# A hybrid decoder layer on one core: the first norm's token sums as single columns in another PSUM bank, and the transposes of the residual in pairs

## The chip, the core and the metric

The kernel runs on one core of a Trainium2 chip. TensorE (PE) multiplies matrices out of SBUF into PSUM, which has eight banks of 2 KiB a partition; VectorE (DVE), ScalarE (ACT) and GpSimd (POOL) do the elementwise work, and SyncE (SP) mainly issues DMA transfers. Each engine has its own stream of instructions, in a fixed order, and waits on semaphores. The metric is the device time of one execution in microseconds (us); lower is better.

## What is computed

One layer of a decoder for 512 tokens of width 2048, in float32:

```python
def hybrid_layer(x, ...):
    h = rmsnorm(x, norm1_w)
    proj = h @ w_in
    ...
    y_sb = stick_breaking_attention(heads(sb_q), heads(sb_k), heads(sb_v))
    y_sc = sc_b * causal_depthwise_conv(sc_c * sc_h, sc_conv_w)
    y_gdn = gdn_mixer(gdn_qkv, gdn_z, gdn_a, gdn_b, gdn_conv_w, gdn_a_log, gdn_dt_bias, gdn_norm_w)
    y = jnp.concatenate([y_sb.astype(x.dtype), y_sc, y_gdn], axis=-1)
    x = x + y @ w_out
    h2 = rmsnorm(x, norm2_w)
    return x + jnp.square(jax.nn.relu(h2 @ w_up)) @ w_down
```

A last rmsnorm follows. The three mixers are six heads of stick-breaking attention, four groups of a short gated convolution and six heads of a gated delta rule (GDN).

## The kernel before

The activations lie transposed in SBUF: 128 features on the partitions, 512 tokens along the free axis, 16 such tiles for the width of 2048. A float32 product is made of three fast ones: each operand is split into a rounded part (`hi`) and a rest (`lo`), and `mm3` (lines 116 to 118) issues hi·hi, hi·lo and lo·hi into one PSUM bank. A `gemm` of one 128-wide output tile is 16 steps of `mm3`, so 48 matmuls of 512 columns; its weights come in four chunks through `wload`: a DMA into `raw`, a cast by ACT into `whi` (line 103), a subtraction by DVE into `wlo` (line 104), with four buffers of each. The outputs of the gemms rotate over three banks named `mm`.

*First norm.* While x is loaded, ACT squares each tile and DVE adds the squares up in `acc` (128 x 512). The products with x run meanwhile without the norm, which is a factor for each token and is put in when results leave PSUM. The factor is wanted in two layouts. `R` (128 x 512, one column for each token, the same in all partitions) comes from one product of `ones` with `acc` (line 221) into the only bank of the tag `r`, and `rsqrt_exp`, two instructions on ACT (lines 146 and 148). `rtok` (128 x 4, tokens on the partitions) comes from four products of a 128-column block of `acc` with the whole matrix `ones` (line 226), again in the bank `r`, of which one column for each block is read. At this moment three gemms are finished and fill all three `mm` banks (`first`); the first of these leaves PSUM with line 344, `xp = p * R` on DVE, and the next gemm takes its bank.

*Mixers.* The GDN heads follow, each a chain of small matmuls (lines 361 to 544) between the many gemms of the input projection; then attention, which begins with `sb_qk(0)` and `sb_attn(0)`. There `sq` and `sk` are cast by ACT out of two `mm` banks (line 582), and the scores `z` are products of the two (lines 116 to 118 with outputs `z`). The last step of the last GDN head just before is line 544, four transposes on PE, whose result ACT scales into `y` (line 546).

*Output projection.* The loop over `m` runs 16 gemms with `wo`. After gemm m, DVE adds the residual and makes `x1[m]` (line 793). The residual is also wanted with tokens on the partitions; `turn(m)` (lines 774 to 777) makes four transposes of `x1[m]` into a bank of the tag `t` (two of them), copies them by ACT into half of the tile `turned`, and after an odd m sends both halves by one DMA to `xs` in DRAM. The loop calls `turn` for m-2 and m-1 ahead of gemm m for even m, and for 14 ahead of gemm 15.

*MLP.* The up and down projections follow, with an algorithm of seven products in place of eight, weights formed on DVE by additions. Its first weights (`q`, 512 KB each) are loaded into the space of the output projection's activations, so their DMAs start when its last gemm ends.

*Order.* Nobody writes the order of the instructions by hand. A scheduler takes instructions by priority (the code's order, with exceptions such as `tc.high_priority`) when their inputs are ready by its own reckoning of time, engine by engine; `behind(ins)` puts what is traced inside it behind `ins` on `ins`'s engine. A change in one place can thus move instructions far away.

Of the kernel before, what the change touches and what calls it, by code (L numbers as in the profile page):

```python
# [2 lines left out]

# [13 lines left out]
P = 128  # L17
T = 512
NB = T // P
D = 2048  # L20
KT = D // P
# [6 lines left out]
CHUNK_KT = 4  # L28
# [26 lines left out]
def trunk(ctx, tc, xT, wv1, wv2, wa, wo, wu, wd, vec, wf, out, dbg=None):  # L55
    nc = tc.nc
    V, S, G, PE = nc.vector, nc.scalar, nc.gpsimd, nc.tensor
# [15 lines left out]
    def mmps():  # L73
        pool, bufs = pool_of_mm
        return pool.tile([P, 512], F32, name="mm", tag="mm", bufs=bufs)

    def xps(tag):
        pool, bufs = pool_of[tag]
        return pool.tile([P, 512], F32, name=tag, tag=tag, bufs=bufs)
# [8 lines left out]
    def tmp(n=512):  # L88
        return per.tile([P, n], F32, name="tmp", tag="tmp", bufs=4)

    def big():
        return big_pool.tile([P, 2, 512], F32R, name="big", tag="big", bufs=16, align_bytes=256)

    def f32t(shape, name):
        return per.tile(shape, F32, name=name)

    def wload(src, n, prio=None):
        with tc.high_priority(WPRIO if prio is None else prio):
            raw = per.tile([P, 512], F32, name="raw", tag="raw", bufs=4)
            nc.sync.dma_start(out=raw[:, :n], in_=src)  # L100
            hi = per.tile([P, 512], F32R, name="whi", tag="whi", bufs=4, align_bytes=256)
            lo = per.tile([P, 512], F32R, name="wlo", tag="wlo", bufs=4, align_bytes=256)
            S.copy(out=hi[:, :n], in_=raw[:, :n])  # L103
            V.tensor_tensor(out=lo[:, :n], in0=raw[:, :n], in1=hi[:, :n].bitcast(F32), op=ALU.subtract)  # L104
        return hi, lo

    def behind(*ins):

        ctx = ExitStack()
        for i in ins:  # L110
            ctx.enter_context(tc.issue_after(i.ins))
        return ctx

    def mm3(p, lh, ll, rh, rl, first, last, more=False):

        PE.matmul(p, lhsT=lh, rhs=rh, start=first, stop=False, skip_group_check=more)  # L116
        PE.matmul(p, lhsT=lh, rhs=rl, start=False, stop=False, skip_group_check=more)  # L117
        return PE.matmul(p, lhsT=ll, rhs=rh, start=False, stop=last, skip_group_check=more)  # L118

    def gemm_chunk(p, src, acts, c, prio=None):  # L120

        ks = slice(c * CHUNK_KT, (c + 1) * CHUNK_KT)
        hi, lo = wload(src[:, ks, :].rearrange("p k f -> p (k f)"), CHUNK_KT * P, prio)
        for k in range(CHUNK_KT):
            s = slice(k * P, (k + 1) * P)
            a = acts[c * CHUNK_KT + k]
            mm3(p, hi[:, s], lo[:, s], a[:, 0], a[:, 1], c + k == 0, c * CHUNK_KT + k == KT - 1)

    def gemm(src, acts):
        p = mmps()  # L130
        for c in range(KT // CHUNK_KT):
            gemm_chunk(p, src, acts, c)
        return p

    def silu(x, s):
# [8 lines left out]
    def rsqrt_exp(o, i, scale, bias):  # L144

        S.activation(out=o, in_=i, func=AF.Ln, scale=scale, bias=eps_c)
        if bias is None:
            S.activation(out=o, in_=o, func=AF.Exp, scale=-0.5)
        else:
            S.activation(out=o, in_=o, func=AF.Exp, scale=-0.5, bias=bias)  # L150
# [8 lines left out]
    ones = f32t([P, P], "ones")  # L159
# [3 lines left out]
    def col(c):  # L163
        return vc[:, c:c + 1]
# [5 lines left out]
    def pt(shape, name, tag=None, bufs=1, dt=F32):  # L170
        return ph_pool.tile(shape, dt, name=name, tag=tag or name, bufs=bufs)
# [15 lines left out]
    acc = big_pool.tile([P, 512], F32, name="acc", tag="acc")  # L187
    pp0 = psum_pool("ps_v", v=4, r=1)
    v1p = [xps("v") for _ in range(NB)]
# [4 lines left out]
    for k in range(KT):  # L194
        hi, lo = wload(wv1[:, k, :], 268, 0)
        xr = big_pool.tile([P, 512], F32, name="xr", tag="xr", bufs=6)
        nc.sync.dma_start(out=xr, in_=xT[:, k, :])
        a = big()
# [4 lines left out]
        for b in range(NB):  # L203
            s = slice(b * P, (b + 1) * P)
# [15 lines left out]
    p = xps("r")  # L220
    PE.matmul(p, lhsT=ones, rhs=acc, start=True, stop=True)
    rsqrt_exp(R, p, 1.0 / D, None)
    rtok = pt([P, NB], "rtok")
    p = xps("r")
    for b in range(NB):
        PE.matmul(p[:, b * P:(b + 1) * P], lhsT=acc[:, b * P:(b + 1) * P], rhs=ones, start=True, stop=True)
    rsqrt_exp(rtok, p.rearrange("p (b f) -> p b f", b=NB)[:, :, 0], 1.0 / D, None)
    rtoks = pt([P, NB], "rtoks")
    S.mul(out=rtoks, in_=rtok, mul=SCALE)

# [84 lines left out]
    p = xps("r")  # L315
# [414 lines left out]
    yh = []  # L730
    for k in ORDER:
        a = big()
# [7 lines left out]
    def half_split(o, src):  # L740
        S.copy(out=o[:, :, 0], in_=src)
        V.tensor_tensor(out=o[:, :, 1], in0=src, in1=o[:, :, 0].bitcast(F32), op=ALU.subtract)
# [8 lines left out]
    def sums(o, A11, A12, A21, A22):  # L751

        sub(o[:, 0], A22, A21)
        nsub(o[:, 1], o[:, 0], A11)
        nsub(o[:, 2], o[:, 1], A12)
        sub(o[:, 3], A11, A21)
# [10 lines left out]
    def turn(m, p=None):  # L767

        if m % 2 == 0:
            turned["o"] = late.tile([P, NB, 2 * P], F32, name="turned", tag="turned", bufs=1)  # L770
        o = turned["o"]
        p = xps("t") if p is None else p
        for b in range(NB):
            PE.transpose(p[:, b * P:(b + 1) * P], x1[m][:, b * P:(b + 1) * P], ident)
        S.copy(out=o[:, :, m % 2 * P:m % 2 * P + P], in_=p.rearrange("p (b f) -> p b f", b=NB))
        if m % 2:
            nc.sync.dma_start(out=xs[:, :, (m - 1) * P:(m + 1) * P], in_=o)
# [7 lines left out]
    for m in range(KT):  # L785
        xr = big_pool.tile([P, 512], F32, name="xr", tag="xr", bufs=6)
        nc.sync.dma_start(out=xr, in_=xT[:, m, :])
        if m == KT - 1 or m and m % 2 == 0:
            for q in range(m - m % 2 - 2 + 2 * (m % 2), m):
                turn(q)  # L790
        p = gemm(wo[m], yh)
        x = big_pool.tile([P, 512], F32, name="x1", tag="xr", bufs=6) if m < KT - 1 else tmp()
        V.tensor_tensor(out=x, in0=p, in1=xr, op=ALU.add)
        y = tmp()
        S.activation(out=y, in_=x, func=AF.Copy, scale=col(C_N2 + m))
        if m == 0:
            S.activation(out=Rb, in_=x, func=AF.Square)
        else:
            sq = tmp()
            S.activation(out=sq, in_=x, func=AF.Square)  # L800
            if m < KT - 1:
                G.tensor_tensor(out=Rb, in0=Rb, in1=sq, op=ALU.add)
        x1.append(x)
        yw.append(y)
        i = m // 2
        half_split(XP[i][:, m % 2:m % 2 + 1], y[:, :HT].unsqueeze(1))
        if m % 2:
            t = xsum = late.tile([P, 4, HT], F32, name="xsum", tag="xsum", bufs=2)
            y0 = yw[m - 1]
            sums(t, y0[:, :HT], y[:, :HT], y0[:, HT:], y[:, HT:])  # L810
            if m < KT - 1:
                rows(i, t, y)
# [437 lines left out]
```

## Time and profile before

| | |
|---|---|
| time, median of 3 runs | 2168.53 us (2166.35 to 2169.36) |
| the profiled execution: its own time | 2170.97 us |
| the profiled execution: its span | 2169.3 us |
| PE busy | 2140.7 us (99%) |
| DVE busy | 1660.4 us (77%) |
| ACT busy | 1073.7 us (49%) |
| mean granted TensorE clock | 0.996 of full speed |

The span goes from the first instruction to the last of the profiled execution; its own time has 1.7 us more around it. Busy shares are means over stages with different limits: the first 740 us are the mixers with the input projection, 740 to 895 us the output projection, 895 to about 1540 us the up projection, and the rest the down projection and the last norm.

### The profile page before, as it was taken

The numbers are of one execution on the slowest core, as the hardware profiler recorded it, in microseconds if no ns is written. First come the engines' busy times: TensorE is split into PE (matmuls) and PEld (weight loads), VectorE is DVE, ScalarE is ACT, GpSimd is POOL, SyncE is SP. The second block draws the span as 40 slices with busy tenths as digits, with TensorE's granted clock in tenths as the row PEclk, the third lists the DMA queues.
The fourth block names the chain that finished last, engine by engine and source line by source line (L and its number), as shares of the span: only waits on it lengthen the run. The fifth ranks groups of instructions, "written<-read, shape, count | busy, mean of one in ns | idle before, by whom it ended". The sixth has DMA issues, their size and how long they took to land.

```text
span 2169.3 us, 33100 instructions
## 1 busy us (share of the span) xinstructions
PE 2140.7 (99%) x12674; PEld 1884.5 (87%) x12674; DVE 1660.4 (77%) x2360; ACT 1073.7 (49%) x1629; POOL 131.8 (6%) x188
## 2 busy tenths in 40 slices
PE   9999999999999999899999999999999999999998
PEld 8887888888988888799999999999878888888886
DVE  6678978644657755477888788778898898898897
ACT  5646666333445544444444454445544444454455
POOL 0000000000000011100000000000001000000101
PEclk9999999999999999899999999999999999999999
DMA  6333232322222354666666665666896877787674
GB/s 184 107 99 95 82 91 91 92 92 84 83 83 83 103 169 150 215 188 196 194 174 187 195 192 172 191 195 181 280 310 182 242 219 196 208 228 226 184 213 117
DMA packets 160719, 356.42 MB, mean 164 GB/s; under 512 B 20273, under 2 KB 62257, under 8 KB 160433
## 3 DMA queue, kind: packets, MB, share of 16 engines
q1 hardware_dynamic: 146304, 302.93, 41.4%
q0 software_dynamic: 13968, 50.86, 13.6%
q8 instruction: 99, 1.62, 0.3%
q14 instruction: 60, 0.48, 0.1%
q10 hardware_dynamic: 288, 0.52, 0.1%
HBM read 308.90 MB, written 45.36 MB: 163 GB/s over the span
## 4 chain that ended last, share of the span: by engine, by line
PE 92%; DVE 3%; DMA 2%; ACT 1%; issue 1%; SPq 0%; DVEq 0%; ACTq 0%
PE mm L117 10%; PE mm L116 10%; PE mm L118 10%; PE pu L118 10%; PE pu L116 10%; PE pu L117 10%; PE pp L117 9%; PE pp L118 9%; PE pp L116 9%; PE mm L280 1%; PE mm L281 1%; PE mm L279 1%; DMA ha<-hs 1%; DVE W L842 1%; DMA q<-in_wu_dram 0%
## 5 line engine op out<-in xcount | busy, mean ns | idle before, releaser
L841 ACT CAST W<-q 128x1024 fp32r<-128x1024 f32 x446 | 466.7, 1054 | 579.4 <-PE pp L118 258.0
L842 DVE TENSOR_TENSOR W<-q,W 128x1024 fp32r<-128x1024 f32 x446 | 540.9, 1221 | 134.8 <-ACT W L841 130.7
L116 PE MATMUL mm<-big,whi 128*128 128x512 f32 x1024 | 404.8, 396 | 1.3 <-ACT whi L103 0.6
L117 PE MATMUL mm<-big,whi 128*128 128x512 f32 x1024 | 403.9, 394 | 0.0
L118 PE MATMUL mm<-big,wlo 128*128 128x512 f32 x1024 | 402.5, 393 | 0.0
L117 PE MATMUL pp<-W,A 128*128 128x512 f32 x888 | 346.1, 390 | 1.0 <-DVE W L842 1.0
L118 PE MATMUL pp<-W,A 128*128 128x512 f32 x888 | 345.7, 389 | 0.4 <-DVE A L842 0.4
L116 PE MATMUL pp<-W,A 128*128 128x512 f32 x888 | 343.3, 389 | 1.4 <-ACT W L841 1.1
L104 DVE TENSOR_TENSOR wlo<-raw,whi 128x512 fp32r<-128x512 f32 (+1 forms) x292 | 196.6, 675 | 158.3 <-ACT whi L103 150.4
L103 ACT CAST whi<-raw 128x512 fp32r<-128x512 f32 (+1 forms) x292 | 177.3, 608 | 276.5 <-PE mm L117 239.0
L116 PE MATMUL pu<-XS,W 128*128 128x256 f32 x1024 | 288.4, 282 | 9.8 <-ACT W L841 9.6
L118 PE MATMUL pu<-XS,W 128*128 128x256 f32 x1024 | 287.7, 281 | 0.5 <-DVE W L842 0.5
L117 PE MATMUL pu<-XS,W 128*128 128x256 f32 x1024 | 287.8, 281 | 0.0
L116 PEld LDWEIGHTS mm<-big,whi 128*128 128x128 f32 x1024 | 192.4, 188 | 41.4 <-ACT whi L103 2.0
L118 PEld LDWEIGHTS mm<-big,wlo 128*128 128x128 f32 x1024 | 192.4, 188 | 39.1 <-DVE wlo L104 0.3
L117 PEld LDWEIGHTS mm<-big,whi 128*128 128x128 f32 x1024 | 192.5, 188 | 39.0 <-DVE big L734 0.3
L116 PEld LDWEIGHTS pu<-XS,W 128*128 128x128 f32 x1024 | 193.8, 189 | 10.8 <-ACT W L841 9.8
L116 PEld LDWEIGHTS pp<-W,A 128*128 128x128 f32 x888 | 166.7, 188 | 37.1 <-ACT W L841 2.5
L117 PEld LDWEIGHTS pp<-W,A 128*128 128x128 f32 x888 | 166.7, 188 | 37.0 <-DVE W L842 2.5
L118 PEld LDWEIGHTS pp<-W,A 128*128 128x128 f32 x888 | 166.7, 188 | 35.3 <-DVE A L842 0.8
L859 DVE TENSOR_TENSOR q<-q 128x1024 f32<-128x1024 f32 x159 | 193.9, 1220 | 2.2 <-DMA q<-in_wd_dram 0.9
L118 PEld LDWEIGHTS pu<-XS,W 128*128 128x128 f32 x1024 | 193.7, 189 | 0.8 <-DVE W L842 0.8
(302 smaller groups left out, 3284.9 us busy)
## 6 DMA issues: line engine op xcount, KB each, us to landing
q<-in_wu_dram SPq DMA_DIRECT2D x128, 512.0 KB, 4.9
q<-in_wd_dram SPq DMA_DIRECT2D x128, 512.0 KB, 5.6
raw<-in_wa_dram SPq DMA_DIRECT2D x192, 256.0 KB, 2.9
hs<-h SPq DMA_DIRECT2D x32, 1024.0 KB, 5.3
q<-in_wd_dram POOLq DMA_DIRECT2D x64, 512.0 KB, 6.9
ha<-hs SPq DMA_DIRECT2D x55, 512.0 KB, 6.6
q<-in_wu_dram POOLq DMA_DIRECT2D x33, 512.0 KB, 5.6
raw<-in_wo_dram SPq DMA_DIRECT2D x64, 256.0 KB, 3.0
```

The costliest lines, as they stand in the source:

```text
L103: S.copy(out=hi[:, :n], in_=raw[:, :n])
L104: V.tensor_tensor(out=lo[:, :n], in0=raw[:, :n], in1=hi[:, :n].bitcast(F32), op=ALU.subtract)
L116: PE.matmul(p, lhsT=lh, rhs=rh, start=first, stop=False, skip_group_check=more)
L117: PE.matmul(p, lhsT=lh, rhs=rl, start=False, stop=False, skip_group_check=more)
L118: return PE.matmul(p, lhsT=ll, rhs=rh, start=False, stop=last, skip_group_check=more)
L279: PE.matmul(o, lhsT=xw[k][:, 0, s], rhs=hi[:, ws], start=k == 0 and b % 2 == 0, stop=False)
L280: PE.matmul(o, lhsT=xw[k][:, 0, s], rhs=lo[:, ws], start=False, stop=False)
L281: PE.matmul(o, lhsT=xw[k][:, 1, s], rhs=hi[:, ws], start=False, stop=k == KT - 1 and b % 2 == 1)
L841: return (S.copy(out=o[:, 0], in_=src), V.tensor_tensor(out=o[:, 1], in0=src, in1=o[:, 0].bitcast(F32), op=ALU.subtract))
L842: V.tensor_tensor(out=o[:, 1], in0=src, in1=o[:, 0].bitcast(F32), op=ALU.subtract))
L859: on_v = lambda t, u: V.tensor_tensor(out=t, in0=t, in1=u, op=ALU.add)
```

## The change

Two edits, and a helper for the second. In the first norm, each of the four products for `rtok` gets one column of `ones` as its moving operand instead of all 128, and writes one column each into `v1p[0][:, 268:272]`, columns that are free in the first of the four banks of the tag `v`. Those banks hold the products for v and the gates (268 columns), which are finished by then and read only with `rtok`. `rsqrt_exp` reads the four columns from there.

In the output projection, the calls of `turn` are handed to `gemm`, which traces them after its second chunk, `behind` the last matmul of that chunk. (`gemm_chunk` now returns that matmul.)

```diff
             a = acts[c * CHUNK_KT + k]
-            mm3(p, hi[:, s], lo[:, s], a[:, 0], a[:, 1], c + k == 0, c * CHUNK_KT + k == KT - 1)
+            last = mm3(p, hi[:, s], lo[:, s], a[:, 0], a[:, 1], c + k == 0, c * CHUNK_KT + k == KT - 1)
+        return last
 
-    def gemm(src, acts):
+    def gemm(src, acts, between=()):
+
         p = mmps()
         for c in range(KT // CHUNK_KT):
-            gemm_chunk(p, src, acts, c)
+            last = gemm_chunk(p, src, acts, c)
+            if c == 1 and between:
+                with behind(last):
+                    for f in between:
+                        f()
         return p
...
-    p = xps("r")
+    p = v1p[0][:, 268:268 + NB]
     for b in range(NB):
-        PE.matmul(p[:, b * P:(b + 1) * P], lhsT=acc[:, b * P:(b + 1) * P], rhs=ones, start=True, stop=True)
-    rsqrt_exp(rtok, p.rearrange("p (b f) -> p b f", b=NB)[:, :, 0], 1.0 / D, None)
+        PE.matmul(p[:, b:b + 1], lhsT=acc[:, b * P:(b + 1) * P], rhs=ones[:, 0:1], start=True, stop=True)
+    rsqrt_exp(rtok, p, 1.0 / D, None)
...
-        if m == KT - 1 or m and m % 2 == 0:
-            for q in range(m - m % 2 - 2 + 2 * (m % 2), m):
-                turn(q)
-        p = gemm(wo[m], yh)
+        turns = range(m - m % 2 - 2 + 2 * (m % 2), m) if m == KT - 1 or m and m % 2 == 0 else ()
+        p = gemm(wo[m], yh, [partial(turn, q) for q in turns])
```

The lines of the changed kernel are 1 to 7 further down; line 116 is 117 there, 544 is 551 and 774 is 781. The scheduler's order changes as follows. In the first norm the four token sums stand where they stood on PE, between line 221 and the next gemm.

In the output projection of the kernel before, on PE, the transposes of `x1[2]` (`x_7497`) stand at the start of gemm 4:

```order
L117 MATMUL mm<-big,whi 128x512
L118 MATMUL mm<-big,wlo 128x512
L774 MATMUL t<-ident,x_7497 128x128 x4
L116 MATMUL mm<-big,whi 128x512
L117 MATMUL mm<-big,whi 128x512
```

and those of `x1[3]` (`x_7581`) 21 matmuls later:

```order
L117 MATMUL mm<-big,whi 128x512
L118 MATMUL mm<-big,wlo 128x512
L774 MATMUL t<-ident,x_7581 128x128 x4
L116 MATMUL mm<-big,whi 128x512
```

In the changed kernel, on PE, the same two (`x_7496` and `x_7580` there) stand together:

```order
L118 MATMUL mm<-big,whi 128x512
L119 MATMUL mm<-big,wlo 128x512
L781 MATMUL t<-ident,x_7496 128x128 x4
L781 MATMUL t<-ident,x_7580 128x128 x4
L117 MATMUL mm<-big,whi 128x512
```

The even tile's transposes moved back by 24 matmuls and the odd tile's by 3, to the middle of gemm 4; so it is for the six pairs from (2, 3) to (12, 13). The pair (0, 1) stays apart, and the transposes of tile 14 move by one matmul. On ACT the two copies of a pair now follow each other, and on SP the DMA to `xs` goes behind one more load of weights. From the end of the last gemm on, the DMA queue has the same transfers in the same order.

At the start of attention, on PE, the kernel before has the transposes of the last GDN head (line 544), six matmuls of the gemm for q of the second attention head, and then the scores `z`:

```order
L118 MATMUL mm<-big,wlo 128x512
L544 MATMUL o<-ident,MT 128x128 x4
L116 MATMUL mm<-big,whi 128x512
L117 MATMUL mm<-big,whi 128x512
L118 MATMUL mm<-big,wlo 128x512
L116 MATMUL mm<-big,whi 128x512
L117 MATMUL mm<-big,whi 128x512
L118 MATMUL mm<-big,wlo 128x512
L116 MATMUL z<-sk,sq 128x512
```

The changed kernel, on PE, has:

```order
L117 MATMUL mm<-big,whi 128x512
L118 MATMUL mm<-big,whi 128x512
L119 MATMUL mm<-big,wlo 128x512
L551 MATMUL o<-ident,MT 128x128 x4
L117 MATMUL z<-sk,sq 128x512
L117 MATMUL z<-sk,sq 128x384
```

The last six matmuls of that gemm moved ahead of the transposes, and `z` now follows the transposes directly. On ACT the order there is `y` (line 546), the casts of `sq` and `sk`, two casts `vhl`, a copy, a cast `whi`, the cast of the next `sq`, and the copy out of the first `sq`'s bank (line 585); the change takes only the cast `whi` out of this row, to ahead of `y`.

Between these places, in the GDN stretch, the small matmuls move by -25 to +42 positions, counted in gemm matmuls. Over PE's whole row up to the up projection, the changes between gemm matmuls and others go from 335 to 331; the six pairs alone take 12 away, so there are eight more, or four more groups of small matmuls, elsewhere. The shortest distance that comes of it is in the last head, on PE, between the products of line 389 (396 in the changed kernel) and those of line 404 (411), which reuse their two banks (tag `i`). Before, 18 gemm matmuls lie between them, the last nine of them these:

```order
L512 MATMUL s<-bp,MT 128x128
L117 MATMUL mm<-big,whi 128x512
L118 MATMUL mm<-big,wlo 128x512
L116 MATMUL mm<-big,whi 128x512
L117 MATMUL mm<-big,whi 128x512
L118 MATMUL mm<-big,wlo 128x512
L116 MATMUL mm<-big,whi 128x512
L117 MATMUL mm<-big,whi 128x512
L118 MATMUL mm<-big,wlo 128x512
L116 MATMUL mm<-big,whi 128x512
L404 MATMUL i<-kq 128x256 x2
```

In the changed kernel there are eight, the last five of them these:

```order
L117 MATMUL mm<-big,whi 128x512
L118 MATMUL mm<-big,whi 128x512
L119 MATMUL mm<-big,wlo 128x512
L470 MATMUL b<-X_925,MT 32x32
L117 MATMUL mm<-big,whi 128x512
L118 MATMUL mm<-big,whi 128x512
L519 MATMUL s<-bp,MT 128x128
L470 MATMUL b<-X_925,MT 32x32 x7
L411 MATMUL i<-kq 128x256 x4
```

The last head's products of line 404 moved up by ten gemm matmuls towards what they wait for.

## Rows read from the trace of the kernel before

**Rows 1.** The page: busy time of PE, the granted clock of TensorE in 40 slices, and the head of the chain that ended last.

```profile
PE 2140.7 (99%) x12674; PEld 1884.5 (87%) x12674; DVE 1660.4 (77%) x2360; ACT 1073.7 (49%) x1629; POOL 131.8 (6%) x188
...
PEclk9999999999999999899999999999999999999999
...
PE 92%; DVE 3%; DMA 2%; ACT 1%; issue 1%; SPq 0%; DVEq 0%; ACTq 0%
```

**Rows 2.** The waits of PE, longest first in total: who waited for whom, us in total, times, longest.

```profile
PE pu L116 <- ACT W L841: 9.6, 1, 9.6
...
PE r L226 <- ACT R L146: 0.8, 1, 0.8
...
PE z L116 <- ACT sk L582: 0.4, 1, 0.4
PE mm L116 <- ACT sq L585: 0.4, 1, 0.4
...
PE mm L116 <- DVE xp L344: 0.2, 1, 0.2
```

**Rows 3.** The timeline of all engines at the end of the first norm: start, us, engine, line, operation, and in brackets the idle time before it and who ended it.

```profile
66.50 1.02 PE L221 MATMUL r<-acc,ones 128*128 128x512 f32 x2
...
67.55 0.69 ACT L146 ACTIVATE R<-r,eps_c 128x512 f32<-128x512 f32 x1 [0.47 <-PE r L221]
...
68.27 0.63 ACT L148 ACTIVATE R<-R 128x512 f32<-128x512 f32 x1
68.29 1.16 PE L226 MATMUL r<-ones,acc 128*128 128x128 f32 x8 [0.78 <-ACT R L146]
68.94 0.69 DVE L344 TENSOR_TENSOR xp<-mm,R 128x512 f32<-128x512 f32 x1 [1.13 <-ACT R L148]
...
69.49 0.26 ACT L146 ACTIVATE rtok<-r,eps_c 128x4 f32<-128x4 f32 x1 [0.59 <-PE r L226]
...
69.68 0.50 PE L116 MATMUL mm<-big,whi 128*128 128x512 f32 x1 [0.23 <-DVE xp L344]
```

**Rows 4.** The timeline of PE around one group of four transposes in the output projection; one row for each matmul, of which the left-out ones run in the same rhythm.

```profile
767.71 0.39 PE L116 MATMUL mm<-big,whi 128*128 128x512 f32 x1
...
781.09 0.39 PE L118 MATMUL mm<-big,wlo 128*128 128x512 f32 x1
781.32 0.60 PE L774 MATMUL t<-ident,x 128*128 128x128 f32 x4
781.67 0.48 PE L116 MATMUL mm<-big,whi 128*128 128x512 f32 x1
781.99 0.39 PE L117 MATMUL mm<-big,whi 128*128 128x512 f32 x1
...
783.15 0.39 PE L116 MATMUL mm<-big,whi 128*128 128x512 f32 x1
```

**Rows 5.** The timeline of PE around ten transposes in a row, in attention.

```profile
732.25 0.39 PE L118 MATMUL mm<-big,wlo 128*128 128x512 f32 x1
732.49 1.25 PE L633 MATMUL z<-ident,zs 128*128 128x128 f32 x10
733.50 0.48 PE L116 MATMUL mm<-big,whi 128*128 128x512 f32 x1
...
734.97 0.39 PE L116 MATMUL mm<-big,whi 128*128 128x512 f32 x1
```

**Rows 6.** ACT's and SP's timelines in the output projection: a cast of weights with the idle time before it, and the DMA to `xs` among the loads.

```profile
881.22 0.62 ACT L103 CAST whi<-raw 128x512 fp32r<-128x512 f32 x1 [2.10 <-PE mm L117]
...
878.63 0.52 SPq L777 DMA_DIRECT2D xs<-turned  x1
879.87 3.05 SPq L100 DMA_DIRECT2D raw<-in_wu_dram  x2
...
895.51 2.49 SPq L849 DMA_DIRECT2D q<-in_wu_dram  x4
```

**Rows 7.** The timeline of all engines at the start of attention.

```profile
526.73 0.60 PE L544 MATMUL o<-ident,MT 128*128 128x128 f32 x4
527.08 0.47 PE L116 MATMUL mm<-big,whi 128*128 128x512 f32 x1
527.36 0.69 ACT L546 ACTIVATE y<-o,vc 128x512 f32<-128x512 f32 x1 [1.40 <-PE o L544]
...
528.41 0.60 ACT L582 CAST sk<-mm 128x512 fp32r<-128x512 f32 x1
...
529.06 0.79 PE L116 MATMUL z<-sk,sq 128*128 128x512 f32 x3 [0.36 <-ACT sk L582]
...
530.24 0.64 ACT L103 CAST whi<-raw 128x512 fp32r<-128x512 f32 x1
...
530.76 0.60 ACT L582 CAST sq<-mm 128x512 fp32r<-128x512 f32 x1
...
530.95 0.28 PE L118 MATMUL z<-sk,sq 128*128 128x256 f32 x1
...
531.24 0.29 ACT L585 COPY sq<-mm 128x128 f32<-128x128 f32 x1
...
531.58 0.50 PE L116 MATMUL mm<-big,whi 128*128 128x512 f32 x1 [0.35 <-ACT sq L585]
```

**Rows 8.** Groups of ACT's instructions by line and shape: count, busy us in total, mean ns of one, idle before.

```profile
L103 ACT CAST whi<-raw 128x512 fp32r<-128x512 f32 x276 | 170.7, 619 | 261.3 <-PE mm L117 226.7 <-PE mm L281 17.0 <-PE v L208 6.1
...
L392 ACT ACTIVATE g<-i 128x512 f32<-128x512 f32 x6 | 3.6, 600 | 0.0
L381 ACT COPY y<-i 128x512 f32<-128x512 f32 x6 | 3.5, 584 | 2.5 <-PE i L380 2.5
```

**Rows 9.** Busy time of each engine in windows of 2 us around PE's longest wait; the number after POOL's is the granted clock, then DMA's share and GB/s.

```profile
900.00:902.00 2.00, 1.62 (x14) 1.38 (x13) 0.00 (x0) 0.34 (x1) 2.00 (x3) 1.00 0.82 281
902.00:904.00 2.00, 0.00 (x0) 0.00 (x0) 0.00 (x0) 0.24 (x1) 0.98 (x1) 1.00 0.97 327
904.00:906.00 2.00, 0.00 (x0) 0.00 (x0) 0.00 (x0) 0.00 (x0) 0.00 (x0) 0.63 1.05 277
...
914.00:916.00 2.00, 2.00 (x11) 2.00 (x11) 1.34 (x2) 0.95 (x2) 0.00 (x0) 0.50 1.03 393
...
918.00:920.00 2.00, 2.00 (x14) 1.59 (x13) 1.62 (x2) 0.98 (x2) 0.00 (x0) 0.96 1.08 409
920.00:922.00 2.00, 2.00 (x19) 2.00 (x18) 1.21 (x1) 1.67 (x3) 0.00 (x0) 1.00 1.03 409
```

More of the change, by code (lines that the diff above doesn't have):

```diff
@@ L2 @@
 from contextlib import ExitStack
+from functools import partial
 import numpy as np
```

## The prediction

> **What bounds the kernel now.** I read the page first [rows 1]: PE is busy for 2140.7 of 2169.3 us, the chain that ended last is PE for 92% of the span, and the granted clock is at its upper level (2.4 GHz) in nearly every slice. So an edit can gain only what PE itself executes or waits. I then read PE's waits [rows 2]. The largest, 9.6 us, is at the start of the up projection, for the first weights of that stage. What touches this change is small: 0.8 and 0.2 us at the first norm, and 0.4 and 0.4 us at the start of attention. The other waits of that list lie outside the stretches whose order moves. DVE and ACT matter only where PE's queue stands for them. The next three views are therefore timelines at the places where the order moved: the first norm [rows 3], the transposes [rows 4 and 5] and the start of attention [rows 7].
>
> **The first norm: nothing.** The rows show two waits around the four token sums, 0.78 us ahead of them (they need bank `r`, which ACT is still reading for `R`) and 0.23 us behind them [rows 3]. The change takes the first away: the sums get a bank of their own and can start when line 221 ends, at 66.50 + 1.02 = 67.52 us. But the gemm behind them doesn't wait for the sums. It waits for `xp` to free its bank, and that chain runs line 221 to 67.52, ACT's two instructions for `R` from 67.55 to 68.27 + 0.63 = 68.90, DVE's `xp` from 68.94 to 69.63, gemm at 69.68 [rows 3]. No link of it is touched. The old sums lie under it (68.29 to 69.45). The new ones, if they cost as much as before (1.16 us for eight passes; one column instead of 128 can hardly cost more), end by 68.68, 0.95 us before `xp` does. The 1.0 us of waiting becomes one wait of at least 1.0 us, all of it for `xp`, and the gemm still starts at 69.68. The term is 0; if that cover were gone, the sums would be worth up to 1.16 us. ACT can make `rtok` right after `R`, at 68.90 in place of 69.49 [rows 3], so the gates of the GDN come about 0.6 us earlier; PE has gemms to run until it needs them, so nobody gains but the scheduler, which fills the stretch in another order.
>
> **The transposes in pairs: -0.2 us.** In the output projection a gemm matmul starts every (781.09 - 767.71) / 59 = 0.227 us [rows 4]. From the last start before the four transposes (781.09) to the seventh gemm start behind them (783.15) it takes 2.06 us, of which seven steps are 1.59, so the group costs 0.47 us. The same sum for ten transposes is 734.97 - 732.25 = 2.72, less 1.59, so 1.13 us [rows 5]. Six more transposes cost 0.66, or 0.11 each; four are 0.44, and what is left for going over to transposes and back is 0.03 us. Six pairs save one such change each: -0.2 us. The saving is at most what the steps after a group are late: from 781.67 to 783.15, 1.48 us for six steps of 0.227, which is 0.12 a group, or -0.7 us; at the other end it is 0. The order makes four more groups of small matmuls in the GDN, at 0.03 to 0.12 each: +0.1 us, at most 0.5.
>
> Nothing else in this stage pays. The odd tile's transposes come 24 matmuls (5.4 us) after the end of the gemm whose sum they read. The second copy on ACT holds a cast of weights up by 0.6 us, and ACT stands idle for 2.1 us before each such cast, waiting for PE to release a buffer [rows 6]. The DMA to `xs` passes one more load of weights on SP, so the last pair's goes out at about 881 in place of 878.6; the loads of the up projection start at 895.5 [rows 6], in unchanged order, so the 9.6 us wait stays.
>
> **The start of attention: +0.9 us.** This is the largest term, and the diff doesn't show it. Before, ACT can begin `y` when the four transposes of line 544 are done; the casts of `sq` and `sk` stand behind `y` on ACT, and `z` on PE needs them [rows 7]. From the transposes' start (526.73) to `z` (529.06) it takes 2.33 us. PE fills 1.36 us of this with the six gemm matmuls in between (6 x 0.227) and waits 0.36. The change puts these six ahead of the transposes. They then start at 526.73 + 1.36 = 528.09, and `z` at 528.09 + 2.33 = 530.42: the wait ahead of `z` grows from 0.36 to about 1.7 us. Some comes back. Before, the next gemm waits 0.35 us for ACT's copy out of the first `sq`'s bank. That copy ends at 531.24 + 0.29 = 531.53, 4.80 us after the transposes start; with the cast `whi` (530.24 to 530.76) gone from ahead of it, 4.28 us. So it ends at 532.37 and the gemm may start at 532.42. By PE's own work, `z` takes 530.95 - 529.06 = 1.89 us to its last start and 0.12 more, which gives 532.43. Either way the gemm resumes at 532.4 against 531.58, with the same work done: +0.85 us. The upper end is 1.36 us, if the second wait doesn't shrink.
>
> **The rest of the GDN stretch: 0, at most +0.6 us.** Small matmuls have moved there, and PE shows no wait before. The tightest new place is line 404 in the last head. It needs two banks, freed by ACT's copy (0.58 us) and exponential (0.60); with one cast of weights (0.62) ahead that is 1.80 us [rows 8]. Eight gemm matmuls are 1.81 us, and eight small ones lie there too. It just fits; a second cast ahead would cost about 0.6 us. I take 0, since the scheduler's order of before shows no wait at any of its tight places.
>
> **Sum.** 0 - 0.2 + 0.1 + 0.9 + 0 = +0.8 us, between -0.7 + 0.1 + 0.85 = +0.2 and 1.36 + 0.5 + 0.6 = +2.5. The profiled execution would go from 2170.97 to 2171.8 us (its span from 2169.3 to 2170.1). It lies 2.4 us above the median of the runs, so I put the difference on the median: 2168.53 + 0.8 = **2169.3 us**. A measurement of this kernel can tell about 0.2%, or 4.3 us, from no change.
>
> **Rivals.** *The waits at the first norm do go away.* If the gemm behind the token sums could start when they end, PE would gain the 0.78 and 0.23 us; with the upper saving for the transposes (0.7) the sum is -1.0 - 0.7 + 0.9, and the time 2167.7 us. For it speaks that the wait is named after bank `r`; against it, that the row of the gemm itself names `xp` [rows 3], and that three gemms hold all three banks. 15%.
>
> *The clock falls at the new wait.* This one ends slower. After the transposes PE would stand for about 1.7 us. In PE's longest wait the granted clock still reads 1.00 from 902 to 904, with PE idle since 901.6; it reads 0.63 in the next 2 us and 0.50 (1.2 GHz) while PE works again, until about 918 [rows 9]. At that level 11 matmuls start in 2 us against 19 [rows 9], so 7 us (911.2 to 918.2) lose 7 x (1 - 11/19) = 2.9 us. If the new wait set this off, the time would be 2168.53 + 0.8 + 2.9 = 2172.2 us. [...] Ten transposes in a row, 1.0 us, left the rhythm of the gemm behind them at 0.23 us [rows 5]. The Trainium skill (TensorE: Matmul & The Clock Gate, section "Part 4: PE-mode transpose") says that transposes don't count as busy for the clock as other matmuls do. By that rule the stretch would begin with the transposes and be 0.35 us longer, 2.0 us, still under the 2.4 us that the rows bear; no run here shows the rule at work. 6%.
>
> *The moved order meets more waits in the GDN*, one of about 0.6 us at several of the heads: 2170.5 to 2172. Against it, no wait there before. 9%.
>
> **How the numbers follow.** The forecast (2169.3) has 70%, the first rival 15, the second 6, the third 9. The runs of before spread by 2.2 below and 0.8 above their median, so with the sum's bounds the forecast's own range is about 2167 to 2171.5. To hold 8 in 10 with the first rival and the third's lower part, I take 2166.3 to 2172.2. Faster by over 0.2% (under 2164.2) needs more than all named gains together: 4%. Slower by over 0.2% (above 2172.9) needs the clock to fall and another wait on top, or several: 6%. Within: 90%.
>
> **What would show it.** In the changed trace the token sums should start at about 67.5 us with no wait, and the next gemm at 69.7 with one wait of 1 us or more on `xp`. `z` should show a wait of about 1.7 us on the cast of `sk`, and the gemm behind it none or under 0.1. The pairs of transposes should cost about 0.9 us together. The first `q` loads of the up projection should start about 0.8 us later than before, and the wait there should be 9.6 us again. The prediction is wrong if the gemm starts ahead of `xp`, if the granted clock falls near 530 us, or if PE's waits between 80 and 520 us add up to more than 1 us.

## The result, and the profile after

The changed kernel takes 2172.57 us (median of 19 runs, 2170.20 to 2175.00), the kernel before 2168.01 (19 runs of the same session, 2166.02 to 2169.46): +4.6 us, a ratio of 1.0022 [1.0016, 1.0029]. It is slower, by 0.2%, and 0.4 us above the range of the prediction. The profiled execution took 2173.73 us, its span is 2172.0.

PE's waits in the changed kernel, columns as in [rows 2]:

```profile
PE pu L117 <- ACT W L846: 9.7, 1, 9.7
...
PE z L117 <- ACT sk L589: 1.7, 1, 1.7
PE b L470 <- DMA X<-sy: 1.5, 1, 1.5
PE mm L117 <- DVE xp L351: 1.4, 1, 1.4
...
PE mm L117 <- DVE tmp L575: 1.2, 1, 1.2
```

The wait for `pu` is as before. The line left out behind it is for weights while x is still loading (1.3 us at 14.8 us in this profile, 0.6 in another of the same kernel), ahead of both edits. Two of the others were forecast (`z` and `xp`). Two are new: `X<-sy` and `tmp`, both in the GDN stretch. Here is the timeline of PE and DVE at the first norm, to be laid beside [rows 3]:

```profile
66.41 1.02 PE L228 MATMUL r<-acc,ones 128*128 128x512 f32 x2
67.27 0.95 PE L233 MATMUL v<-ones,acc 128*128 128x1 f32 x8
68.85 0.69 DVE L351 TENSOR_TENSOR xp<-mm,R 128x512 f32<-128x512 f32 x1 [1.13 <-ACT R L155]
69.59 0.50 PE L117 MATMUL mm<-big,whi 128*128 128x512 f32 x1 [1.38 <-DVE xp L351]
...
70.41 0.63 PE L117 MATMUL mm<-big,whi 128*128 128x512 f32 x1
```

The sums start without a wait, and the gemm behind them at 69.59 (69.68 before), after one wait of 1.38 us for `xp`. That is the forecast. But 0.8 us later each matmul takes 0.63 us. The windows of 2 us show why (the number after POOL's is the granted clock):

```profile
68.00:70.00 2.00, 0.62 (x4) 0.49 (x5) 1.15 (x5) 1.78 (x6) 1.04 (x1) 1.00 0.43 128
70.00:72.00 2.00, 2.00 (x7) 1.60 (x6) 1.84 (x6) 1.97 (x7) 0.00 (x0) 0.59 0.07 26
72.00:74.00 2.00, 2.00 (x6) 1.54 (x6) 1.45 (x3) 0.12 (x2) 0.10 (x1) 0.56 0.64 240
74.00:76.00 2.00, 2.00 (x10) 1.64 (x9) 0.88 (x3) 1.97 (x4) 0.00 (x0) 1.00 0.00 0
```

The clock is at its lower level (1.2 GHz) from 70.3 to 73.8, while PE works: 6 or 7 matmuls in 2 us in place of 10.

*The wait for X.* In each GDN head, DVE's chain ends with `Yq`; SP stores it to DRAM (`sy`), and four loads bring it back as `X`, on which line 470 (463 before) works. In between, SP also issues `Bq`, the next head's load. SP's issues in the kernel before:

```profile
151.80 0.34 SPq L451 DMA_DIRECT2D sy<-Yq  x1
152.71 0.53 SPq L440 DMA_DIRECT2D Bq<-sm  x1
...
153.96 1.81 SPq L455 DMA_DIRECT2D X<-sy  x4
```

And in the changed kernel, with PE's row for `X`:

```profile
152.67 0.53 SPq L447 DMA_DIRECT2D Bq<-sm  x1
...
153.94 0.36 SPq L458 DMA_DIRECT2D sy<-Yq  x1
...
158.01 1.74 SPq L462 DMA_DIRECT2D X<-sy  x4
...
160.07 0.24 PE L470 MATMUL b<-X,MT 32*32 32x32 f32 x2 [1.46 <-DMA X<-sy]
```

`sy` was issued 0.9 us ahead of `Bq`, and is now issued 1.3 us behind it. DVE ends its last step on `Yq` at 152.57, so the store stands 1.4 us ready behind two loads (`Bq` and one of weights). Then it also takes longer to land. The view of the DMA issues from 150 to 162 us has, for each, its size and the median time from issue to landing. Before:

```profile
Bq<-sm SPq DMA_DIRECT2D x1, 512.0 KB, 4.5
...
sy<-Yq SPq DMA_DIRECT2D x1, 64.0 KB, 1.5
```

After:

```profile
sy<-Yq SPq DMA_DIRECT2D x1, 64.0 KB, 4.1
```

So `X` is issued 4.07 us after `sy`, where it was 2.16, and PE waits 1.46 us. The Trainium skill (DMA: Bandwidth & Descriptors, section "Queues, rings and completion order") says that each DMA engine takes descriptors of one ring in ring order, and that SP issues all its transfers on one row of rings. The 4.1 us behind two loads, against 1.5 ahead of them, agree with that.

*The wait for tmp.* DVE and PE at the end of the GDN stretch:

```profile
482.81 2.10 DVE L580 SCALAR_TENSOR_TENSOR y<-tmp,vc,y 128x512 f32<-128x512 f32 x3
484.83 0.68 DVE L575 TENSOR_TENSOR tmp<-mm,tmp 128x512 f32<-128x512 f32 x1
485.57 0.50 PE L117 MATMUL mm<-big,whi 128*128 128x512 f32 x1 [1.15 <-DVE tmp L575]
```

Line 575 reads an `mm` bank that the next gemm needs. DVE has put three taps of the short convolution (line 580, 2.10 us) ahead of it; before, line 575's twin (568) ran ahead of the taps, and PE had no such wait.

*The start of attention*, beside [rows 7]:

```profile
532.62 0.60 PE L551 MATMUL o<-ident,MT 128*128 128x128 f32 x4
533.25 0.69 ACT L553 ACTIVATE y<-o,vc 128x512 f32<-128x512 f32 x1
...
534.31 0.60 ACT L589 CAST sk<-mm 128x512 fp32r<-128x512 f32 x1
...
534.96 0.79 PE L117 MATMUL z<-sk,sq 128*128 128x512 f32 x3 [1.74 <-ACT sk L589]
```

From the transposes to `z` it takes 2.34 us (2.33 before), of which PE now waits 1.74. The granted clock stays at its upper level here in this execution.

### The profile page after: what moved, and what is told of

Read it like the earlier page. It is cut to its first block, busy times and chain, and to the rows that moved or that the text cites. A ratio compares the mean times of both kernels' runs of the same rounds, so it can differ in the third digit from the quotient of the medians.

```text
span 2172.0 us, 33096 instructions
## 1 busy us (share of the span) xinstructions
PE 2138.2 (98%) x12674; PEld 1883.6 (87%) x12674; DVE 1660.7 (76%) x2360; ACT 1071.9 (49%) x1629; POOL 132.9 (6%) x188
## 4 chain that ended last, share of the span: by engine, by line
PE 92%; DVE 3%; DMA 3%; ACT 1%; issue 1%; SPq 0%; DVEq 0%; ACTq 0%
PE mm L117 10%; PE mm L118 10%; PE mm L119 10%; PE pu L119 10%; PE pu L117 10%; PE pu L118 10%; PE pp L118 9%; PE pp L119 9%; PE pp L117 9%; PE mm L287 1%; PE mm L288 1%; PE mm L286 1%; DMA xq<-xs 1%; DMA q<-in_wu_dram 0%; PE i L411 0%
```

## Where the time goes, for all kernels

The order of small matmuls among the gemms differs, but each kernel issues the same 3456 matmuls of the `mm` gemms ahead of the up projection. The table gives the start of the n-th of them less that of the kernel before, with the difference at the 120th (61 us, ahead of the first norm's sums) taken as zero (all counted from 0). At each count in the table the changed kernel has done the same small matmuls as before (218, 532, 892 and 907 in the profiles, the first norm's sums in their new shape), so none of a difference is small matmuls that stand earlier or later; between these counts it swings by up to 2 us for that reason. Each row is one profile. Three profiles whose order up to the output projection is that of before (e2, e6, e9) spread from -0.4 to +0.3, nearly all of it at the place of X.

| kernel | 180th (78 us), behind the first norm | 960th (292), behind X | 1800th (523), behind tmp | 1860th (540), behind z | last (895), behind the pairs | wait for X |
|---|---|---|---|---|---|---|
| changed | 1.61 | 3.58 | 4.60 | 5.48 | 5.22 | 1.5 |
| changed again (e11) | 1.60 | 3.08 | 4.10 | 4.95 | 4.72 | 1.0 |
| norm alone (e1) | 0.01 | 1.47 | 2.47 | 3.34 | 3.34 | 1.0 |
| norm alone again (e12) | 1.57 | 3.14 | 4.13 | 4.99 | 5.01 | 1.0 |
| one column, old bank (e3) | 0.04 | 2.10 | 3.12 | 4.00 | 3.98 | 1.6 |
| changed, four products more (e4) | 0.00 | 1.21 | 2.22 | 3.08 | 2.81 | 0.7 |
| changed, 61 columns (e5) | 0.02 | 1.00 | 2.02 | 4.37 | 4.11 | 0.5 |
| changed, z pinned (e7) | 1.53 | 3.02 | 3.99 | 4.01 | 3.73 | 0.8 |
| changed, SP pinned (e8) | 1.61 | 1.06 | 1.05 | 1.04 | 0.77 | none |
| e8, four products more (e10) | 0.04 | -0.29 | -0.29 | -0.29 | -0.57 | none |
| norm, order of before (e6) | 0.00 | -0.42 | -0.42 | -0.42 | -0.42 | none |
| both, order of before (e9) | 0.00 | -0.03 | -0.04 | -0.03 | -0.29 | none |
| pairs alone (e2) | 0.01 | 0.34 | 0.33 | 0.32 | 0.03 | 0.2 |

Behind 895 us the executions part by what the granted clock does at the start of the up projection, which differs from execution to execution (the profile of before is at the lower level from 904.5 to 918.2 us, that of the changed kernel from 910.0 to 920.3), and at the start of the down projection (e1, e6 and e9, below), so single profiles aren't compared there.

## The experiments

### One edit at a time: e1 and e2

e1 has the first norm's edit alone:

```diff
-    p = xps("r")
+    p = v1p[0][:, 268:268 + NB]
...
-        PE.matmul(p[:, b * P:(b + 1) * P], lhsT=acc[:, b * P:(b + 1) * P], rhs=ones, start=True, stop=True)
+        PE.matmul(p[:, b:b + 1], lhsT=acc[:, b * P:(b + 1) * P], rhs=ones[:, 0:1], start=True, stop=True)
```

> The first norm's edit alone; the transposes stay apart as before. My theory: the loss comes with this edit, by three parts of the changed trace: the granted clock falls behind the longer wait for xp (3.4 us at half rate, 1.7 us lost), and the order that the scheduler makes of the mixers meets waits that were not there (1.4 us on a DMA in the first head, 1.15 us on a bank, 0.9 us at the start of attention). It expects 4 to 5 us over the kernel before, about 2172.5, with those waits in the trace. The rival, that the pairs of transposes and what follows them cost the time, expects less than 1 us over it.

Measured: 2173.07 against 2167.49 us, ratio 1.0024 [1.0015, 1.0034]. Its profile has the waits for X (1.0), `tmp` (1.1), `z` (1.7) and `xp` (1.4), but the clock stays at its upper level at 70 us: that part of the expectation was missed in this execution.

e2 has the output projection's edit alone (`gemm(..., between)` and the calls of `turn` handed to it, as in the change's diff).

> The transposes in pairs alone; the first norm as before, so the order up to the output projection is that of before. My theory: 0.2 to 0.3 us gained at the pairs, about 2167.7, which a timing can't tell from no change; the gemms of the output projection drift by -0.28 us against before, and the waits of the mixers are those of before. The rival expects 3 to 5 us more than before.

Measured: 2167.57 against 2167.49, ratio 1.0003 [0.9994, 1.0011]. All of the loss comes with the first norm's edit. What the pairs do is read from the table's last two columns: the nine rows with pairs, in whatever order, gain 0.23 to 0.29 us between the 1860th matmul and the end of the output projection; the four rows without them (e1, e12, e3, e6) gain -0.02 to 0.02.

### Which part of the first norm's edit: e3, e4, e6

e3 keeps the old bank and takes only the single columns (no pairs):

```diff
-    p = xps("r")
+    p = xps("r")[:, 0:NB]
...
-        PE.matmul(p[:, b * P:(b + 1) * P], lhsT=acc[:, b * P:(b + 1) * P], rhs=ones, start=True, stop=True)
+        PE.matmul(p[:, b:b + 1], lhsT=acc[:, b * P:(b + 1) * P], rhs=ones[:, 0:1], start=True, stop=True)
```

> The first norm's sums as single columns, but still in the bank r, and no pairs in the output projection. The order in the mixers is then that of the changed kernel but for a few rows (seven on DVE, five on ACT), while the wait ahead of the sums for R stays as before. Theory (the loss is the moved order of the mixers, and the order moves because the sums are shorter, whatever their bank): the waits at X of head 0 (1.0 to 1.5 us), at the bank behind tmp (1.1) and at z (1.7) are there again, the up projection starts 3 us late, and the time is about 2171, 3 us above before. Rival (the loss comes from the first norm itself, from the sums in the other bank and the one long wait behind them): no loss, 2168.

Measured: 2173.78 against 2167.34, ratio 1.0029 [1.0017, 1.0041], so a loss of 3.7 to 8.9 us where 3 was expected. Its profile has the old split wait at the first norm (0.8 and 0.3 us), no fall of the clock there, and the waits for X, tmp and z (1.6, 1.2, 1.7). So neither the bank nor the one long wait is needed for the loss: the shorter sums move the scheduler's order, and the order costs 4.0 us in the table. The rival falls.

e4 is the changed kernel with four more products behind the token sums, into columns that nobody reads; the order is otherwise that of the changed kernel:

```diff
+    for i in range(4):
+        PE.matmul(v1p[1][:, 268:396], lhsT=ones, rhs=ones, start=True, stop=True)
```

> The changed kernel with four more products of ones by ones behind the token sums, whose result nobody reads; they fill the wait for xp, and the order of everything else is that of the changed kernel. If the longer wait lets the clock fall, the granted clock stays at the upper level around 70 us here, the gemm behind the wait starts at the same 69.6, and 1.7 us come back: about 2170.9. If the clock's fall there is chance or costs nothing, the time is that of the changed kernel, 2172.6. The waits later in the mixers stay in both cases.

Measured: 2171.45 against 2167.49, ratio 1.0018 [1.0009, 1.0027]. The time can't decide between the two forecasts: the interval holds the changed kernel's 1.0022 too. The profile can. The wait for `xp` is 0.4 us, the clock stays up, and nothing is lost at the first norm (0.00 in the table); the moved order's waits are all there.

e6 has the new sums in the new bank with six such products ahead of them, and no pairs. The scheduler then gives exactly the order of before.

> The new token sums (single columns in the other bank) with six products of ones by ones ahead of them that nobody reads, and no pairs; with these the scheduler makes exactly the order of the kernel before. If the moved order and the clock are the whole loss, the time is that of before, 2168.0, give or take 0.5, with no new wait in the mixers. If the new place or the single columns cost something themselves, it is nearer 2172.

Measured: 2168.70 against 2167.49, ratio 1.0002 [0.9993, 1.0011]. The new sums in the order of before lose nothing that can be measured, and no wait for X or tmp is left.

### Which places of the order: e7, e8

e7 is the changed kernel with the last two steps of the gemm for the second head's q held behind the last of the last GDN head's transposes (`T5`, passed to `gemm` as `after`), as before:

```diff
+            with behind(*((after,) if after is not None and c * CHUNK_KT + k >= KT - 2 else ())):
+                last = mm3(p, hi[:, s], lo[:, s], a[:, 0], a[:, 1], c + k == 0, c * CHUNK_KT + k == KT - 1)
...
-        qk[h] = sb_split(gemm(wa[24 + 2 * h], xw), "sq") + sb_split(gemm(wa[24 + 2 * h + 1], xw), "sk")
+        qk[h] = sb_split(gemm(wa[24 + 2 * h], xw, after=pin.get('T5') if h == 1 else None), "sq") + sb_split(gemm(wa[24 + 2 * h + 1], xw), "sk")
```

> The changed kernel with one place put back: the last six matmuls of the gemm for q of the second attention head are held behind the four transposes of the last GDN head, as before. Theory: the wait at z falls from 1.7 to 0.4 us, the gemm behind z starts 0.9 us earlier against the changed kernel, nothing moves ahead of it, and the time is about 0.9 us under the changed kernel's (2171.7 against 2172.6). Rival (the wait comes back at the copy out of the first sq's bank, 0.35 us before): the gain is 0.5 us or less.

Measured: 2171.87 against 2167.34, ratio 1.0022 [1.0013, 1.0031]. Beside the kernel before of the same session that is +4.5 us, where the changed kernel was +4.6: by time the two can't be told apart. The profile can. The wait at `z` is 0.3 us, the one at the copy of `sq` 0.4 as before, and from the 1800th to the 1860th matmul the loss grows by 0.02 us where the changed kernel's grows by 0.88. The term of the start of attention is worth 0.9 us.

e8 is the changed kernel with the second head's `Bq` held behind the first head's `sy` on SP:

```diff
-        nc.sync.dma_start(out=B.rearrange("p a b -> p (a b)"),
-                          in_=sm.rearrange("k a b -> k (a b)").unsqueeze(1).broadcast_to([16, 8, 1024]))
+        with behind(*((gb["sy"],) if h == 1 else ())):
+            nc.sync.dma_start(out=B.rearrange("p a b -> p (a b)"),
+                              in_=sm.rearrange("k a b -> k (a b)").unsqueeze(1).broadcast_to([16, 8, 1024]))
...
-        nc.sync.dma_start(out=sy.rearrange("k c a -> (k c a)").rearrange("(p f) -> p f", p=P),
+        gb["sy"] = nc.sync.dma_start(out=sy.rearrange("k c a -> (k c a)").rearrange("(p f) -> p f", p=P),
```

> The changed kernel with the load Bq of the second head's matrices held behind the store sy of the first head on SP's queue, so that a store that is ready no longer stands behind a load that waits for another transfer. The scheduler makes another order behind this place. Theory: PE's wait for X in the first head (1.5 us) goes to under 0.3, and up to the gemm matmuls of that place the loss against before goes from 3.4 to about 2 us (with a clock fall at 70 us) or from 1.0 to about 0 (without). What the rest of the order does isn't foreseen; without new waits the time is 1 to 1.4 us under the changed kernel's. Rival (X is late because DVE's chain Yq ends later, not because of the queue): the wait stays at 1 us.

Measured: 2167.70 against 2167.34, ratio 0.9998 [0.9989, 1.0007]. SP's issues are in the old sequence:

```profile
151.03 0.34 SPq L459 DMA_DIRECT2D sy<-Yq  x1
151.55 0.53 SPq L448 DMA_DIRECT2D Bq<-sm  x1
153.57 1.74 SPq L463 DMA_DIRECT2D X<-sy  x4
```

`sy` lands 2.5 us after its issue, and PE doesn't wait for X in this head. The rival (DVE's chain) falls. But the kernel is 0.4 us above the kernel before of its session, where the changed one is 4.6 above: 4.2 us come back, not 1 to 1.4. With this one transfer in its old place the scheduler's order falls back into that of before (PE's matmuls are the same as with the pairs alone from the 1102nd of the profile's 12674 on), and the waits for tmp and z go as well. So e8 shows what one place decides, and doesn't price X alone; X's price is the wait that the profiles show, 0.5 to 1.6 us. The fall of the clock at 70 us is still there (1.61 in the table).

### Both edits without the moved order: e9, e10

e9 has both edits and e6's six products ahead of the sums.

> Both edits, with six products of ones with ones ahead of the token sums into columns that nobody reads. With them the scheduler gives the mixers exactly the order of before. Theory (the order is the loss, the pairs give 0.3 us): no wait at X, tmp and z beyond those of before, output projection 0.3 us shorter, time 0.3 us under before, ratio 0.9995 to 1.0003, 4 us under the changed kernel. Rival (the edits themselves cost something together): 2170 or more.

Measured: 2167.45 against 2167.34, ratio 1.0000 [0.9992, 1.0009]. No wait for X or `tmp` is left, and the rival (2170 or more) falls.

e10 is e8 with e4's four products.

> The changed kernel with the store sy ahead of the load Bq on SP's queue (as in the run before with that pin) and four products of ones with ones behind the token sums, into columns that nobody reads; the order is otherwise that of the run with the pin alone. Theory (two separate losses, the moved order, which the pin takes away, and a fall of the granted clock behind the long wait for xp, which the products take away): the wait at xp is 0.4 us, the clock stays at its upper level around 70 us, the up projection starts 1.6 us earlier against before than with the pin alone (1.5 us ahead of before), and the time is 2166 to 2167.5. Rival (the clock fall at 70 us is paid back later, in a wait that gets shorter): the up projection starts as with the pin alone, and the time is 2167.7 again.

Measured: 2166.61 against 2167.30, ratio 0.9996 [0.9987, 1.0005]. The wait for `xp` is 0.4, the clock stays up at 70 us, and the up projection starts 1.3 us earlier than in e8 by the table. Beside the kernel before of its session it is 0.7 us lower, where the changed kernel is 4.6 higher. It is the lowest median of all, and can't be told from before.

### The fall of the clock: e11, e12, e5

> The changed kernel once more, unaltered, for a second profile. Theory: the waits of the moved order are fixed and come again (X 1.0 to 1.5 us, tmp 1.1, z 1.7, xp 1.4). The fall of the granted clock at 70 us isn't fixed: the wait for xp was 1.4 us in four profiles and the clock fell in three of them. Rival (the fall belongs to the wait and comes every time): it comes again.

Measured: 2174.18 us, with the waits for X, tmp, z and xp of 1.0, 1.2, 1.7 and 1.4, and the clock at its lower level from 69.5 to 72.9 us.

> The first norm's edit alone once more, unaltered, for a second profile. Its first one showed the wait of 1.4 us for xp without a fall of the clock. Theory (the fall is a matter of the execution, not of the kernel): it may come this time; if so, the up projection starts 1.6 us later than in the first profile, at 4.8 us behind before. Rival (this kernel has something that the changed one lacks, which keeps the clock up): no fall, and the up projection 3.2 us behind before again.

Measured: 2174.18 us; this time the clock fell, from 69.2 to 72.6, and the up projection starts 5.0 us behind by the table, against 3.3 in e1. The same kernel does both. Of the six profiles with a wait of 1.4 us for `xp` (changed, e1, e7, e8, e11, e12) five show the fall, each for 3.4 us and at a price of 1.5 to 1.6 us. It came between 0.1 us ahead of PE's next matmul behind the wait (e7) and 1.2 us after it (e8).

e5 is the changed kernel with 61 columns in each sum, in exactly its order:

```diff
-    p = v1p[0][:, 268:268 + NB]
+    p = v1p[0][:, 268:268 + NB * 61]
...
-        PE.matmul(p[:, b:b + 1], lhsT=acc[:, b * P:(b + 1) * P], rhs=ones[:, 0:1], start=True, stop=True)
+        PE.matmul(p[:, b * 61:b * 61 + 61], lhsT=acc[:, b * P:(b + 1) * P], rhs=ones[:, 0:61], start=True, stop=True)
```

> The changed kernel with 61 columns in each token sum in place of one, in the same other bank, of which one is read as before; the order of all engines is exactly that of the changed kernel. What is open: whether the granted clock falls behind the first norm because PE waits 1.4 us for xp, or because eight products of one column stand ahead of that wait as well. Theory (the wait): the wait is still about 1.3 us, the clock falls at about 70 us in the profile, as in five of six with that wait, 1.6 us are lost there, and the time is the changed kernel's, 2172.6. Rival (the single columns count as idle): no fall, the matmuls behind the first norm start as in before, and the time is about 1.3 us less, 2171.3. The waits of the moved order (X 0.7 to 1.5, tmp 1.1, z 1.7) come in either case.

Measured: 2171.53 against 2167.33, ratio 1.0021 [1.0012, 1.0030]. There is no fall at the first norm behind a wait of 1.33 us. But there is one at `z`, in the windows around and behind its wait (529.6 to 531.35):

```profile
530.00:532.00 2.00, 0.65 (x3) 0.48 (x3) 1.48 (x3) 2.00 (x5) 0.00 (x0) 1.00 0.27 86
532.00:534.00 2.00, 1.95 (x9) 1.70 (x8) 2.00 (x5) 1.46 (x5) 0.00 (x0) 0.67 0.12 45
534.00:536.00 2.00, 2.00 (x7) 1.52 (x6) 1.50 (x3) 0.27 (x1) 0.88 (x3) 0.50 0.00 0
```

It costs 1.5 us (2.35 from the 1800th to the 1860th in the table, against 0.88). Whether single columns count as idle stays open: one profile without a fall isn't enough, since e1 with single columns had none either.

The length of a wait alone doesn't tell whether the clock falls. The same 1.74 us at `z` stand in seven profiles, of which only e5 has a fall there; the 1.5 and 1.6 us for X (changed, e3) have none. And shorter waits can have one. At the start of the down projection PE waits twice for weights (`W`), in e6, e9 and e3 for 1.05 and 0.45 us each. In e6 and e9, which have the order of before, the clock falls behind them for 3.4 us (from 1589.0 and 1585.7 us), in e3 it doesn't; in e1 it falls there too, from 1594.1, behind 1.35 and 0.44 us. From the profile of e9:

```profile
1584.43 0.50 PE L117 MATMUL pp<-W,A 128*128 128x512 f32 x1 [1.05 <-ACT W L848]
1585.37 0.55 PE L117 MATMUL pp<-W,A 128*128 128x512 f32 x1 [0.45 <-ACT W L848]
...
1586.71 0.63 PE L117 MATMUL pp<-W,A 128*128 128x512 f32 x1
```

```profile
1586.00:1588.00 2.00, 2.00 (x6) 1.52 (x6) 2.00 (x3) 0.27 (x1) 0.00 (x0) 0.50 1.05 305
```

## Why the prediction was wrong

The forecast was +0.8 us; the measurement is +4.6. By its steps:

*The first norm: nothing.* The mechanism was right: the wait stayed, as one for `xp`, and the gemm started at 69.59. The first rival (the waits go away) is refuted by the same row. What failed is the assumption that a wait moved together costs what it cost in pieces. Before, 0.78 and 0.23 us stood on either side of the sums; now 1.38 us stand in one place, and in five of six profiles the clock falls behind them, for 1.6 us.

*The clock falls at the new wait*, the second rival, had its mechanism right. It failed on the place, `z` instead of the first norm, and on the chance, for which it set the wait against PE's longest one. [rows 9] show how long the clock reads 1.00 after PE went idle, not how short an idle time is followed by a fall. In the changed kernel PE had been at work again for 0.75 us (from 69.59) when the clock fell at 70.3. Falls came behind 1.4 us at the first norm, 1.74 us at `z` (e5), and 1.05 and 0.45 us in a row (e6, e9); behind the 0.8 us at the first norm (before, e2, e3) none came. The price forecast (2.9 us) was for a longer stretch; it is 1.5 to 1.6.

*The transposes in pairs: -0.2 us.* Right: 0.23 to 0.29, or 0.04 to 0.05 for each of the six groups saved. The upper end of 0.7 was not reached.

*The start of attention: +0.9 us.* Right: 1.74 us of wait, 0.88 lost, and 0.9 given back by e7.

*The rest of the GDN stretch: 0, at most +0.6 us.* This is the step that failed. I looked at one place, line 404, where PE needs banks that ACT frees, and took 0 "since the scheduler's order of before shows no wait at any of its tight places". That says nothing of another order. The waits came at two places that I hadn't followed: X, where the order of SP's queue changed, and `tmp`, where DVE's changed. PE waits 1.46 and 1.15 us there, 2.6 together, so the prediction's own test (over 1 us between 80 and 520 us) is met. In the table the GDN stretch costs 2.0 us behind X and 1.0 behind `tmp` in the changed kernel's first profile, 1.5 and 1.0 in its second. About 0.5 of the first is in no wait, in every profile of the moved order (0.5 to 0.7). Ahead of the 960th matmul these orders have five more groups of small matmuls than before (131 changes against 121 in the profiles), an estimated 0.2 us at the price that the pairs showed, of which the prediction had put +0.1 in its sum; the rest is open, and is of the size by which equal orders differ. The third rival (more waits in the GDN, 2170.5 to 2172) named the mechanism, but as about 0.6 us at several heads and not as 1.5 and 1.15 us at two places; I gave it 9%, and not together with the second.

*Sum.* In the second profile of the changed kernel: 1.6 (clock) + 1.5 + 1.0 (GDN) + 0.85 (`z`) - 0.23 (pairs) = 4.7 us, beside 4.6 in the medians. The same sum without the clock is 3.1, and the first profile gives 5.2, so that the second comes so near to the medians is partly luck.

One thing was shown only in part: that the taps ahead of line 575 cause the wait for `tmp` is read from the rows and from the orders in which it runs ahead of them (before, e6, e8, e9), none of which shows the wait; no run changed that place alone.

## What to carry to other kernels

Where a scheduler lays out a stretch anew because some small work got cheaper, compare the new order of every queue, SP's and DVE's too, at each place where another engine waits for it; that the old order had no waits is no evidence for the new one. A transfer that others wait for belongs ahead of a large load on the same queue: here it paid twice behind it, with 1.4 us until its issue and 2.6 more from issue to landing. Before two short waits of PE are merged into one of over a microsecond, ask what that does to the granted clock behind it, and fill the gap if it costs nothing.

## What the runs showed of the hardware

The granted clock fell behind a PE wait of 1.4 us in five profiles of six, behind one of 1.74 us in one of seven, and behind waits of 1.05 and 0.45 us in a row in two of three; in all but one of these (e7) PE was already at work again. It then stayed at 1.2 GHz for 3.4 us, which cost 1.5 to 1.6 us at the first norm and at `z`. The same kernel shows it in one execution and not in another (e1, e12). A store of 64 KB landed 1.5 us after its issue ahead of a load of 512 KB (2.5 in e8), and 4.1 us after it behind one of 512 and one of 256 KB. Eight passes with one moving column took 0.95 us, with 61 columns 1.00, with 128 columns 1.16 [rows 3]: fewer columns save 0.2 us at most here.
